# Rotary products and input sums of squares moved off GpSimd in a two-layer hybrid decoder

## The chip, the cores and the metric

The kernel runs on one core of a Trainium2 chip. A core has five engines, each with its own queue that is worked off in order: TensorE (PE: matrix products; its weight loads are shown as PEld), VectorE (DVE), ScalarE (ACT), GpSimd (POOL) and SyncE (SP), which here only issues transfers. They meet through semaphores. The metric is the device time of one execution in microseconds (us), the median of several runs.

## The reference

Sixteen learned tokens are put ahead of 1024 input tokens of width 1024 (T = 1040), all in float32. Each of two layers does this:

```python
hn = rms_norm(h, norm_mix_g[l])
proj = hn @ w_in[l]
q, k, v, xr, gate = jnp.split(proj, splits, axis=-1)
q = apply_partial_rope(rms_norm(q, q_norm_g[l]), cos, sin)
k = apply_partial_rope(rms_norm(k, k_norm_g[l]), cos, sin)
o_attn = diff_attention(q, k, v, lam)          # 4 heads x 2 components of 64, causal
o_rec = rg_lru_branch(xr, gate, ...)           # conv4, gates, linear recurrence over T
h = h + jnp.concatenate([rms_norm(o_attn), rms_norm(o_rec)], -1) @ w_out[l]
hn = rms_norm(h, norm_ffn_g[l])
h = h + (silu(g) * u) @ w_down[l]              # g, u = hn @ w_gu[l], width 2816
```

`rms_norm` divides each token by the root of the mean of its squares. `apply_partial_rope` turns the first 16 of each 64 dimensions: `x*cos` plus the swapped half times `sin`.

## The kernel before

Activations lie transposed: 128 channels on the partitions, tokens along the free dimension, eight blocks of 128 channels for the width. Work on tokens goes in three chunks of 348, 348 and 344 (`CH`). A float32 product is made from two rounded parts: a high part (`hn0h`, `wh`) and the rest (`hn0l`, `wl`), and three matmuls: high x high, low x high, high x low. `split` makes the two: ScalarE copies the high part, VectorE subtracts for the low part (with a norm weight in one instruction, line 341; without, line 323).

**The start.** `start` loads the input in nine groups (three chunks, each with blocks 0 to 2, 3 to 5 and 6 to 7) into tiles `hr`. Its inner function `group` (line 2159) splits each block into `hn0h` and `hn0l`, then squares the group's tile in place and adds its blocks together, 348 wide. What remains is summed over the channels by TensorE (`st_r`), VectorE makes the reciprocal root of it (`ms_r`, `nq_r`, `rr`), TensorE spreads it over partitions (`bc_r`), and ScalarE stores it as `row`. The first projections (`pxr`) need only `hn0h` and `hn0l`; the norm's factor is multiplied in behind them. `SQP = 2` says that chunks 0 and 1 have their squares and their sums on GpSimd; chunk 2 has squares on ScalarE and sums on VectorE.

**The recurrence** follows with `pxr` and `pgt` (x and gate branch, four blocks each) and small gate products `pga`.

**The rotation.** For each head, `qk_unit` projects a query unit and a key unit of 128 columns (`pq`, `pk`). Its `evac` (line 1008) works per chunk: ScalarE squares the result for the norm and copies it to `craw`; VectorE swaps halves into `csh` (stream shuffle, line 1024); then two products, `csh` times sine (line 1027) and `craw` times cosine (line 1028), on the engine that `ROPE_ENG` names; then VectorE adds them and the split or the key's scaling follows. There are 2 layers x 4 heads x 2 units x 3 chunks = 48 such pairs. Attention itself: TensorE makes scores (`S`), VectorE adds the mask and keeps the maximum (line 1158), ScalarE takes exponentials, VectorE combines both components, TensorE transposes (`atr`) and multiplies with the values (`pvo`). `W_ENG = "G"` puts the low parts of 70 weight halves (`wl`) on GpSimd. GpSimd also issues transfers.

**The order of the work** is set before the program is built. `Planner` runs generators against an estimated clock of each engine; an operation is written out at the moment when its generator is due, so every engine's queue follows from estimated costs (`tt`, `act`, `mm`) and from `S.turn(engine)`, which holds a generator back while that engine's estimated queue is long. Changing the engine of an operation changes the estimates, and with them the order on all engines.

Of the kernel before, what the change touches and what calls it, by code (L numbers as in the profile page):

```python
# [12 lines left out]
AF = mybir.ActivationFunctionType  # L13
ALU = mybir.AluOpType
# [10 lines left out]
CW = 348  # L25
# [55 lines left out]
NSQ, PSTAT = 3, 3  # L81

GATE_AT = 3
SQP = 2
EARLY = [6, 102]
KY = 2
NP1 = 1
# [13 lines left out]
TURN = {"w": (300.0, 3000.0), "q": (300.0, 1.0e9), "k": (0.0, 1.0e9), "v": (300.0, 300.0),  # L103
        "o": (800.0, 1.0e9), "r": (300.0, 1.0e9), "f": (300.0, 1.0e9), "d": (4000.0, 1.0e9), "s": (0.0, 1.0e9)}
DMA_RATE, DMA_END = 360.0, 900.0
ROPE_ENG, W_ENG = "G", "G"
MZ = CW
WY = [T, T, NB * P, NB * P]

# [155 lines left out]
def trunk_kernel(ctx: ExitStack, tc: tile.TileContext, h0, win, wout, wgu, wdn,  # L265
                 wgate, vec, lamd, cosd, sind, maskd, identd, seld, out):
    nc = tc.nc
    V, A, G, PE = nc.vector, nc.scalar, nc.gpsimd, nc.tensor
    S = Planner()
# [17 lines left out]
    def cols(ap):  # L287
        n = 1
        for d in ap.shape[1:]:
            n *= d  # L290
        return n

    def ready(eng, cost, after=0.0):
        return S.busy(eng, cost, after) + LAGS[eng] - LAT

    def aps(*xs):
        return sum(x is not None and not isinstance(x, (int, float)) for x in xs)

    def in_psum(ap):
        return getattr(ap, "space", None) == PSUM  # L300
# [12 lines left out]
    def act(out_, in_, func, after=0.0, **kw):  # L313
        A.activation(out=out_, in_=in_, func=func, **kw)  # L314
        n = aps(kw.get("scale"), kw.get("bias")) + ("accum_out" in kw)
        load = 0.0
        if func in TABLES and TABLES[func] != table[0]:
            table[0], load = TABLES[func], 1280.0
        m = cols(in_)
        return ready("A", max(m * 0.833 + (50 if in_psum(in_) else 93), m * 1.01 + 4) + 94 * n + load, after)  # L320

    def tt(out_, in0, in1, op, after=0.0, eng="V"):
        (V if eng == "V" else G).tensor_tensor(out=out_, in0=in0, in1=in1, op=op)  # L323
        n = cols(out_)
        if eng == "V":
            if not (in_psum(in0) or in_psum(in1)):
                after = S.behind(after)
            return ready(eng, n * 1.042 + 68, after)
        e = ready(eng, n * 2.1 + 148, after)
        S.shared.append((S.clock["G"] - n * 2.1 - 148, S.clock["G"]))  # L330
        return e
# [14 lines left out]
    def dma(eng, out_, in_, nbytes):  # L346
        eng.dma_start(out=out_, in_=in_)  # L347
        start = S.busy("G", 1040.0) + 700 if eng is G else S.busy("H", 450.0) + 770
        return S.busy("D", nbytes / DMA_RATE, start) + DMA_END
# [476 lines left out]
    def new_row(name):  # L826
        return const.pool.tile([P, TP], F32, tag="row", name=name)

    def load_vec(l):
        t = const.pool.tile([P, NVEC], F32, tag="vec", name=f"vec{l}")  # L830
        return t, dma(nc.sync if l else nc.gpsimd, t, vec[l], 512 * NVEC)
# [664 lines left out]
    def open_layer(L):  # L1496
        L.cy = open_pool(f"y{L.l}", "right")
        L.cr = open_pool(f"rec{L.l}", "right")
        L.ca = open_pool(f"attA{L.l}")
        L.accy = Acc(L.cr, L.cr.pool.tile([P, TP], F32, tag="accy", name=f"accy{L.l}"), f"accy{L.l}")  # L1500
        S.start(layer_vectors(L))
        S.set(L.ev_rec)
        S.set(L.ev_open)
# [636 lines left out]
    def start():  # L2140
        L = layers[0]
        L.vt, _ = load_vec(0)
        warm = yield from S.get(small, "d", 1, [P, 4, 4], F32, "warm")
        G.memset(warm, 0.0)
        S.free(act(warm, warm, AF.Exp), warm)
        open_layer(L)
        dma(nc.gpsimd, ident, identd, 512 * P)
        dma(nc.gpsimd, sums0, seld, 2048)
        acc = Parts(3)
        L.row = new_row("row0")  # L2150
        L.r = yield from S.get(small, "rr", 2, [BQ, NB], F32, "rr0")
        L.re = yield from S.get(small, "re", 2, [BQ, 2, NB], F32, "re0")
        _, L.ev_r, L.ev_row = row_stats(acc, KB, 1024.0, "r0", L.r, L.row, L.re)
        for b in range(KB):
            hi = yield from S.get(bpool, "b", 16, [P, T], F32R, f"hn0h{b}")
            lo = yield from S.get(bpool, "b", 16, [P, T], F32R, f"hn0l{b}")
            L.hn[b].parts = (hi, lo)

        def group(c, b0, n, tile_, there):
            t = tile_[:, :3 * CW]  # L2160
            c0, cw = CH[c]
            s = slice(c0, c0 + cw)
            for b in range(b0, b0 + n):
                yield there[b - b0]
                src = t[:, (b - b0) * CW:(b - b0) * CW + cw]
                e = yield from split(L.hn[b].parts[0][:, s], L.hn[b].parts[1][:, s], src,
                                     L.vt[:, V_MIX + b:V_MIX + b + 1])
                S.set(L.hn[b].ev[c], e + LAT)
            sq = t[:, :n * CW]
            if c < SQP:  # L2170
                e = tt(sq, sq, sq, ALU.mult, eng="G")
            else:
                yield from S.turn("A")
                e = act(sq, sq, AF.Square)
            for b in range(1, n):
                yield e + LAT
                e = tt(t[:, :CW], t[:, :CW], t[:, b * CW:(b + 1) * CW], ALU.add, eng="V" if c == 2 else "G")
            acc.put(c, b0 // 3, tile_, e + LAT)

        for c, (c0, cw) in enumerate(CH):  # L2180
            for i, (b0, n) in enumerate(((0, 3), (3, 3), (6, 2))):
                pl, tag, bufs = HR[3 * c + i]
                t = yield from S.get(L.cy if pl == "y" else L.cr, tag, bufs, [P, NB * P if pl == "y" else TP], F32,
                                     f"hr{b0}{c}")
                if cw < CW:
                    G.memset(t[:, :3 * CW].rearrange("p (b t) -> p b t", b=3)[:, :n, cw:], 0.0)
                there = []
                for a, m in ((0, 1), (1, n)) if c == 0 and i == 0 else ((0, n),):
                    e = dma(nc.sync, t[:, :3 * CW].rearrange("p (b t) -> p b t", b=3)[:, a:m, :cw],
                            h0[b0 + a:b0 + m, :, c0:c0 + cw].rearrange("b p t -> p b t"), 512 * cw * (m - a))  # L2190
                    there += [e] * (m - a)
                    if c == 0 and i == 0:
                        if not a:
                            S.start(weights())
                        yield S.now
                S.start(group(c, b0, n, t, there), there[0])
                if c == 0 and i == 2:
                    S.set(ev_x)
                    yield S.now
# [174 lines left out]
```

## Time and profile before

| | us |
|---|---|
| median of 3 timed runs | 2355.84 (2353.6 to 2357.2) |
| the profiled execution | 2362.03 |
| its span, first to last instruction | 2359.3 |
| busy: TensorE, VectorE, ScalarE, GpSimd | 2275.6, 1858.9, 1072.9, 423.1 |
| start, up to the first gate projection | 0 to 55 |
| recurrence of layer 0 | 55 to 138 |
| attention of layer 0, layer 1 | 138 to 470, 1300 to 1650 |

Times in the profile's rows are microseconds from the span's start, then the duration; in rows of groups, the busy time and the mean duration in ns. The clock of TensorE as granted is shown as a share of full speed (PEclk). Square brackets tell how long the engine stood before the row and who ended that.

### The profile page before, as it was taken

The numbers are of one execution on the slowest core, as the hardware profiler recorded it, in microseconds if no ns is written. First come the engines' busy times: TensorE is split into PE (matmuls) and PEld (weight loads), VectorE is DVE, ScalarE is ACT, GpSimd is POOL, SyncE is SP. The second block draws the span as 40 slices with busy tenths as digits, with TensorE's granted clock in tenths as the row PEclk, the third lists the DMA queues.
The fourth block names the chain that finished last, engine by engine and source line by source line (L and its number), as shares of the span: only waits on it lengthen the run. The fifth ranks groups of instructions, "written<-read, shape, count | busy, mean of one in ns | idle before, by whom it ended". The sixth has DMA issues, their size and how long they took to land.

```text
span 2359.3 us, 40740 instructions
## 1 busy us (share of the span) xinstructions
PE 2275.6 (96%) x14514; PEld 2110.9 (89%) x14514; DVE 1858.9 (79%) x4392; ACT 1072.9 (45%) x2090; POOL 423.1 (18%) x611
## 2 busy tenths in 40 slices
PE   7999899989999999999999989989899999999998
PEld 6999898989999999999999989978688888888887
DVE  7889888788888877755877988977888887776565
ACT  4656665453333333444547556644533333334432
POOL 4144333001121101000000442330012221100000
PEclk8999999999999999999999989999999999999999
DMA  3114337234565423756521143372345654238554
GB/s 123 62 39 118 103 87 254 66 122 140 202 213 182 154 93 115 250 180 211 181 93 55 56 121 83 86 252 69 113 139 205 210 189 146 98 130 290 179 189 155
DMA packets 186539, 339.36 MB, mean 144 GB/s; under 512 B 54120, under 2 KB 75290, under 8 KB 186336
## 3 DMA queue, kind: packets, MB, share of 16 engines
q1 hardware_dynamic: 153760, 227.57, 30.5%
q0 software_dynamic: 32576, 109.19, 12.7%
q8 instruction: 114, 1.87, 0.3%
q14 instruction: 89, 0.73, 0.1%
HBM read 219.72 MB, written 95.64 MB: 134 GB/s over the span
## 4 chain that ended last, share of the span: by engine, by line
PE 83%; DVE 11%; issue 2%; ACT 2%; DMA 1%; POOL 0%; SPq 0%; DVEq 0%; ACTq 0%; POOLq 0%
PE pd L304 29%; PE pb L304 16%; PE pa L304 13%; PE pxr L304 4%; PE po L304 3%; PE pgt L304 3%; PE pq L304 3%; PE pvo L304 2%; PE S L304 2%; DVE P L1158 2%; PE pk L304 2%; PE pv L304 1%; PE atr L308 1%; PE pga L304 1%; DVE P L341 1%
## 5 line engine op out<-in xcount | busy, mean ns | idle before, releaser
L304 PE MATMUL pd<-rf,wh 128*128 128x260 f32 (+1 forms) x1848 | 414.4, 319 | 0.0
L304 PEld LDWEIGHTS pd<-rf,wh 128*128 128x128 f32 x1848 | 305.7, 188 | 27.5
L304 PE MATMUL pd<-rf,wl 128*128 128x260 f32 (+1 forms) x924 | 295.9, 320 | 0.0
L347 POOL DMA_DIRECT2D ad<-ct x154 | 83.0, 540 | 577.0 <-DVE ct L323 570.5
L304 PEld LDWEIGHTS pd<-rf,wl 128*128 128x128 f32 x924 | 173.8, 188 | 13.8
L314 ACT ACTIVATE P<-P,mx,cq 116x116 f32<-116x116 f32 (+5 forms) x144 | 124.6, 867 | 79.3 <-DVE mx L341 67.6
L323 DVE TENSOR_TENSOR ct<-pd,ct 128x260 f32<-128x260 f32 (+1 forms) x204 | 102.7, 513 | 71.1 <-PE pd L304 70.9
L304 PE MATMUL pa<-B11h,fA 128*128 128x260 f32 (+1 forms) x528 | 128.4, 324 | 19.1 <-ACT B11h L314 19.1
L323 DVE TENSOR_TENSOR ct<-pb,ct 128x260 f32<-128x260 f32 (+1 forms) x198 | 101.7, 514 | 52.5 <-PE pb L304 49.0
L323 POOL TENSOR_TENSOR wl<-wr,wh 128x512 fp32r<-128x512 f32 x70 | 99.4, 1436 | 156.1 <-ACT wh L314 109.2
L304 PE MATMUL pb<-T2h,fS 128*128 128x260 f32 (+1 forms) x528 | 126.8, 322 | 0.0
L304 PE MATMUL pb<-T1h,fS 128*128 128x260 f32 (+1 forms) x528 | 126.1, 321 | 0.0
L304 PE MATMUL pa<-B21h,fA 128*128 128x260 f32 (+1 forms) x528 | 125.7, 320 | 0.4 <-ACT ct L314 0.4
L304 PE MATMUL pd<-T3h,fS 128*128 128x260 f32 (+1 forms) x528 | 126.1, 320 | 0.0
L304 PE MATMUL pb<-B22h,fS 128*128 128x260 f32 (+1 forms) x528 | 125.6, 319 | 0.0
L304 PE MATMUL pd<-T4h,fA 128*128 128x260 f32 (+1 forms) x528 | 125.2, 319 | 0.0
L323 DVE TENSOR_TENSOR ct<-ct,ct 128x520 f32<-128x520 f32 (+2 forms) x171 | 116.2, 684 | 6.5 <-DMA ad<-ct 2.8
L304 PEld LDWEIGHTS pa<-B11h,fA 128*128 128x128 f32 x528 | 90.6, 192 | 27.7 <-ACT B11h L314 19.8
L314 ACT ACTIVATE ah<-atr 116x348 fp32r<-116x348 f32 (+1 forms) x144 | 57.4, 406 | 88.6 <-PE atr L308 43.7
L304 PEld LDWEIGHTS pb<-T2h,fS 128*128 128x128 f32 x528 | 90.0, 190 | 7.8
L304 PEld LDWEIGHTS pa<-B21h,fA 128*128 128x128 f32 x528 | 88.9, 188 | 8.5 <-ACT ct L314 0.9
L304 PEld LDWEIGHTS pd<-T3h,fS 128*128 128x128 f32 x528 | 89.0, 188 | 8.0
(392 smaller groups left out, 7099.8 us busy)
## 6 DMA issues: line engine op xcount, KB each, us to landing
wr<-in_win_dram SPq DMA_DIRECT2D x80, 256.0 KB, 2.8
ad<-ct POOLq DMA_DIRECT2D x77, 260.0 KB, 2.6
ad<-ct POOLq DMA_DIRECT2D x77, 256.0 KB, 3.0
ct<-in_wgu_dram SPq DMA_DIRECT2D x64, 256.0 KB, 3.1
ht<-in_wgu_dram SPq DMA_DIRECT2D x60, 256.0 KB, 4.1
sq<-ad SPq DMA_DIRECT2D x58, 260.0 KB, 5.1
sq<-ad SPq DMA_DIRECT2D x58, 256.0 KB, 5.2
hw<-in_wgu_dram SPq DMA_DIRECT2D x48, 256.0 KB, 2.8
```

The lines of the kernel that those rows point to most:

```text
L304: PE.matmul(out_, lhsT=lhsT, rhs=rhs, start=start, stop=stop, **(dict(skip_group_check=True) if on else {}))
L308: PE.transpose(out_, in_, idn)
L314: A.activation(out=out_, in_=in_, func=func, **kw)
L323: (V if eng == "V" else G).tensor_tensor(out=out_, in0=in0, in1=in1, op=op)
L341: V.scalar_tensor_tensor(out=out_, in0=in0, scalar=s, in1=in1, op0=op0, op1=op1)
L347: eng.dma_start(out=out_, in_=in_)
L1158: V.tensor_tensor_reduce(out=pt[:mq, k0:k0 + kw], in0=sc[:mq, :kw], in1=mask, scale=1.0, scalar=NEG if i == 0 else mx[:mq, cc, i - 1:i], o ...
```

## The change

The rotation's two products go to VectorE (`ROPE_ENG`), and in `group` all squares go to ScalarE and all sums to VectorE, each behind a `turn` for that engine.

```diff
-SQP = 2
...
-ROPE_ENG, W_ENG = "G", "G"
+ROPE_ENG, W_ENG = "V", "G"
...
             sq = t[:, :n * CW]
-            if c < SQP:
-                e = tt(sq, sq, sq, ALU.mult, eng="G")
-            else:
-                yield from S.turn("A")
-                e = act(sq, sq, AF.Square)
+            yield from S.turn("A")
+            e = act(sq, sq, AF.Square)
             for b in range(1, n):
                 yield e + LAT
-                e = tt(t[:, :CW], t[:, :CW], t[:, b * CW:(b + 1) * CW], ALU.add, eng="V" if c == 2 else "G")
+                yield from S.turn("V")
+                e = tt(t[:, :CW], t[:, :CW], t[:, b * CW:(b + 1) * CW], ALU.add)
             acc.put(c, b0 // 3, tile_, e + LAT)
```

VectorE's queue in the start, from the sixth row on. `hr_124`, `hr_133` and `hr_135` are the three groups of chunk 0, `hn0l_115` to `hn0l_123` the low parts of blocks 3 to 7, `wl_139` a weight. Before:

```order
L341 SCALAR_TENSOR_TENSOR hn0l_115<-hr_133,vec_87,hn0h_114 128x348
L323 TENSOR_TENSOR wl_139<-wr_0_140,wh_138 128x512
L341 SCALAR_TENSOR_TENSOR hn0l_121<-hr_135,vec_87,hn0h_120 128x348
L323 TENSOR_TENSOR wl_139<-wr_1_142,wh_138 128x512
L341 SCALAR_TENSOR_TENSOR hn0l_117<-hr_133,vec_87,hn0h_116 128x348
L341 SCALAR_TENSOR_TENSOR hn0l_123<-hr_135,vec_87,hn0h_122 128x348
L341 SCALAR_TENSOR_TENSOR hn0l_109<-hr_144,vec_87,hn0h_108 128x348
L341 SCALAR_TENSOR_TENSOR hn0l_119<-hr_133,vec_87,hn0h_118 128x348
```

In the changed kernel:

```order
L321 TENSOR_TENSOR hr_124<-hr_124 128x348
L339 SCALAR_TENSOR_TENSOR hn0l_115<-hr_133,vec_87,hn0h_114 128x348
L321 TENSOR_TENSOR hr_124<-hr_124 128x348
L339 SCALAR_TENSOR_TENSOR hn0l_121<-hr_135,vec_87,hn0h_120 128x348
L339 SCALAR_TENSOR_TENSOR hn0l_117<-hr_133,vec_87,hn0h_116 128x348
L321 TENSOR_TENSOR wl_139<-wr_0_140,wh_138 128x512
L339 SCALAR_TENSOR_TENSOR hn0l_123<-hr_135,vec_87,hn0h_122 128x348
L321 TENSOR_TENSOR wl_139<-wr_1_142,wh_138 128x512
L339 SCALAR_TENSOR_TENSOR hn0l_119<-hr_133,vec_87,hn0h_118 128x348
L321 TENSOR_TENSOR hr_135<-hr_135 128x348
```

Sums of squares now stand between the low parts, the first of them ahead of block 3's, and block 4's low part (`hn0l_117`) has moved ahead of the weight.

VectorE's queue at the first two query chunks of layer 0 in the changed kernel (`sin_474` and `cos_473` are the tables, `hs_2` a block of the recurrence):

```order
L1022 STREAM_SHUFFLE cshq_01_1461<-crawq_01_1446 128x348
L321 TENSOR_TENSOR cshq_00_1443<-cshq_00_1443,sin_474 128x348
L321 TENSOR_TENSOR crawq_00_1399<-crawq_00_1399,cos_473 128x348
L321 TENSOR_TENSOR cshq_01_1461<-cshq_01_1461,sin_474 128x348
L321 TENSOR_TENSOR crawq_01_1446<-crawq_01_1446,cos_473 128x348
L321 TENSOR_TENSOR hs_2_1429<-hs_2_1429,gt_20_1104 128x348
```

The four products stood in GpSimd's queue before, ahead of two weight conversions:

```order
L323 TENSOR_TENSOR cshq_00_1436<-cshq_00_1436,sin_461 128x348
L323 TENSOR_TENSOR crawq_00_1404<-crawq_00_1404,cos_460 128x348
L323 TENSOR_TENSOR cshq_01_1461<-cshq_01_1461,sin_461 128x348
L323 TENSOR_TENSOR crawq_01_1448<-crawq_01_1448,cos_460 128x348
L1014 MEMSET csqq_02_1498 128x4
L323 TENSOR_TENSOR wl_1493<-wr_0_1393,wh_1492 128x512
L323 TENSOR_TENSOR wl_1493<-wr_1_1444,wh_1492 128x512
```

TensorE's queue at the first scores of head 0 in layer 0 (`S_0010`, `S_0000`), before, where they stand between the query products of head 1:

```order
L304 MATMUL pq_11_1982<-hn0l_115,wh_1655 128x348
L304 MATMUL pq_11_1982<-hn0h_114,wl_1656 128x348
L304 MATMUL S_0010_2016<-kl_0_1497,view_1836 116x116 x2
L304 MATMUL S_0000_2019<-kh_0_1496,view_1836 116x116 x2
L304 MATMUL pq_11_1982<-hn0h_116,wh_1655 128x348
```

In the changed kernel they stand 49 rows further down, between the key products of head 1:

```order
L302 MATMUL pk_10_2069<-hn0h_114,wl_1906 128x348
L302 MATMUL S_0010_2107<-kl_0_1492,view_1846 116x116 x2
L302 MATMUL S_0000_2110<-kh_0_1491,view_1846 116x116 x2
L302 MATMUL st_q_12_2114<-sums_86,csqq_12_2083 116x2 x3
L302 MATMUL pk_10_2069<-hn0h_116,wh_1905 128x348
```

TensorE's order in both feed-forward stages is the same in the two kernels.

## The prediction

> **What bounds the kernel now.** I read the chain of work that ended last, then the busy time by stage, then the timelines of the two stages that the change touches.
>
> ```profile
> PE 83%; DVE 11%; issue 2%; ACT 2%; DMA 1%; POOL 0%; SPq 0%; DVEq 0%; ACTq 0%; POOLq 0%
> ...
> core 0: us, PE busy (x) PEld busy (x) DVE busy (x) ACT busy (x) POOL busy (x), PEclk, DMA share, GB/s
> 0.00:55.00 55.00, 37.99 (x209) 35.69 (x210) 42.57 (x84) 24.18 (x44) 26.89 (x30) 0.81 0.40 130
> 55.00:138.00 83.00, 82.86 (x523) 82.58 (x522) 64.77 (x100) 59.49 (x85) 14.61 (x14) 1.00 0.16 52
> 138.00:470.00 332.00, 315.40 (x2166) 306.11 (x2164) 289.92 (x1039) 186.29 (x444) 111.92 (x141) 0.98 0.39 117
> 548.00:1196.00 648.00, 648.00 (x5409) 648.00 (x5408) 493.77 (x956) 244.84 (x455) 70.66 (x131) 1.00 0.52 175
> 1300.00:1650.00 350.00, 327.43 (x2101) 308.03 (x2101) 297.31 (x1035) 191.02 (x447) 116.28 (x142) 0.96 0.38 112
> ```
>
> TensorE sets the pace, and VectorE is the only other engine with a real share of the chain. The feed-forward stage (548 to 1196) has TensorE busy for all of its 648 us, and the change leaves its order alone. What can move is the first 55 us, where TensorE is busy for 38.0, and the two attention stages (138 to 470, 1300 to 1650), where it stands 16.6 + 22.6 = 39.2 us. Between 55 and 138 it has no gap, so a lead won before 55 is carried to 138.
>
> At the start, TensorE waits for VectorE's low halves of the input, `hn0l`:
>
> ```profile
> 11.70 0.43 PE L304 MATMUL pxr<-hn0l,wh 128*128 128x348 f32 x1 [1.80 <-DVE hn0l L341]
> 14.62 0.66 PE L304 MATMUL pxr<-hn0l,wh 128*128 128x348 f32 x1 [2.19 <-DVE hn0l L341]
> 17.19 0.66 PE L304 MATMUL pxr<-hn0l,wh 128*128 128x348 f32 x1 [1.33 <-DVE hn0l L341]
> 17.64 0.49 PE L304 MATMUL pxr<-hn0h,wl 128*128 128x348 f32 x1
> 17.93 0.49 PE L304 MATMUL pxr<-hn0h,wh 128*128 128x348 f32 x1
> ...
> 23.59 0.32 PE L304 MATMUL pxr<-hn0h,wh 128*128 128x348 f32 x1
> 23.75 0.32 PE L304 MATMUL pxr<-hn0l,wh 128*128 128x348 f32 x1
> ...
> 35.16 0.66 PE L304 MATMUL pxr<-hn0l,wh 128*128 128x348 f32 x1 [5.59 <-DVE hn0l L341]
> ...
> 39.97 0.38 PE L304 MATMUL pxr<-hn0h,wl 128*128 128x348 f32 x1
> ...
> 54.77 0.32 PE L304 MATMUL pgt<-hn0h,wh 128*128 128x348 f32 x1
> ```
>
> The waits are 1.80, 2.19, 1.33 and 5.59 us. The matmuls also show two paces: 0.29 us apart at 17.64, and 0.16 apart at 23.59 after unbroken work. After the 5.59 us gap the slow pace returns until 39.97, which is 4.8 us at about half speed. The gap thus costs its 5.59 and about 4.8 x (1 - 0.16/0.29) = 2.2 more.
>
> Why is `hn0l` late? VectorE and GpSimd side by side:
>
> ```profile
> 8.11 2.37 DVE L323 TENSOR_TENSOR wl<-wr,wh 128x512 fp32r<-128x512 f32 x1 [0.18 <-ACT wh L314]
> 10.41 1.23 DVE L341 SCALAR_TENSOR_TENSOR hn0l<-hr,vec,hn0h 128x348 fp32r<-128x348 f32 x1
> 12.90 0.57 DVE L341 SCALAR_TENSOR_TENSOR hn0l<-hr,vec,hn0h 128x348 fp32r<-128x348 f32 x1
> 13.39 0.68 DVE L323 TENSOR_TENSOR wl<-wr,wh 128x512 fp32r<-128x512 f32 x1
> 14.00 11.96 DVE L341 SCALAR_TENSOR_TENSOR hn0l<-hr,vec,hn0h 128x348 fp32r<-128x348 f32 x11
> 39.48 2.11 DVE L323 TENSOR_TENSOR hr<-hr 128x348 f32<-128x348 f32 x3
> ...
> 8.02 4.42 POOL L323 TENSOR_TENSOR hr<-hr 128x1044 f32<-128x1044 f32 x3 [4.70 <-DVE hn0l L341]
> 17.21 4.54 POOL L323 TENSOR_TENSOR hr<-hr 128x1044 f32<-128x1044 f32 x3 [0.46 <-DVE hn0l L341]
> ```
>
> The same 128x512 subtraction takes 0.68 us at 13.39 and 2.37 at 8.11, while GpSimd squares `hr`. The eleven `hn0l` from 14.00 take 11.96 us; at the 0.49 of 12.90 to 13.39 they would take 5.4. VectorE stands while GpSimd runs its two-input product. Setting each VectorE instruction against the median of its form without GpSimd beside it, 16 of them (8.11 the first, 39.48 the last) lose 16.0 us to the squares and sums.
>
> **The change at the start.** It removes all of that from GpSimd: six squares and ten sums in the first two thirds of the tokens (the last third already had its squares on ScalarE, its sums on VectorE). ScalarE gets the six squares, VectorE the ten sums:
>
> ```profile
> 7.45 0.63 ACT L314 ACTIVATE wh<-wr 128x512 fp32r<-128x512 f32 x1 [0.15 <-DMA wr<-in_win_dram]
> 8.83 0.58 ACT L314 ACTIVATE hn0h<-hr,vec 128x348 fp32r<-128x348 f32 x1 [0.75 <-DMA hr<-in_h_dram]
> ...
> L314 ACT ACTIVATE hr<-hr 128x1044 f32<-128x1044 f32 x2 | 2.2, 1078 | 4.3 <-DVE hn0l L341 4.3
> L314 ACT ACTIVATE hr<-hr 128x696 f32<-128x696 f32 x1 | 0.8, 783 | 1.2 <-DVE hn0l L341 1.2
> ...
> 243.78 0.92 DVE L323 TENSOR_TENSOR crawk<-crawk,bck 128x348 f32<-128x348 f32 x2
> ```
>
> ScalarE: 4 x 1.08 + 2 x 0.78 = 5.9 us, hidden in the 30.8 us of the first 55 in which this engine stands; without that cover each would put off the high half behind it by about its own 1.08. VectorE: two 348-wide operations together take 0.92, so one takes 0.51 alone and 0.42 behind another; ten cost 4.2 to 5.1 us against 16.0 removed. The first sum of a group now waits for ScalarE's square, with `hn0l` and weight halves queued behind it for which TensorE waits. No DMA issue of the start is moved past another.
>
> I walk the new order with these durations. ScalarE ends `wh` at 8.1, squares `hr` until 9.1, and then makes the fourth block's high half until 9.6 (it had to wait for the DMA until 8.83 anyway). VectorE does the first sum at 9.1 to 9.6, then that block's `hn0l` to 10.2: TensorE goes on at 10.3 instead of 11.70. One more sum and two `hn0l` (0.42 + 2 x 0.49) bring the next one to 11.7 instead of 14.62. Two weight subtractions (0.61 each), two `hn0l` and ScalarE's pieces between give 13.9 instead of 17.19. That is 3.3 us. From there TensorE needs 2.7 us for the 8 matmuls left of the block at 0.29 and carries on; the block on which it stood at 35.16 is made by VectorE directly behind the first rows of the norm, at about 23.5 by the same counting, and TensorE needs it at about 25.8. So the 5.59 and the 2.2 go too: 3.3 + 7.8 = 11.1. Against it: the sums of the second third are ready at about 29.4, when TensorE wants them, and VectorE stands with work behind the norm's first row until TensorE has finished its column sums. I take 1 us for these and forecast **-10 us**. Bounds: -3.3 if a gap like the fourth comes back, -12 if neither of the two costs anything.
>
> **The change in attention.** 96 products (sine and cosine, 3 chunks of 8 query and key units of both layers) go from GpSimd to VectorE:
>
> ```profile
> L323 POOL TENSOR_TENSOR wl<-wr,wh 128x512 fp32r<-128x512 f32 x70 | 99.4, 1436 | 156.1 <-ACT wh L314 109.2 <-DVE wh L335 18.5 <-DMA both<-qh 10.5
> L323 POOL TENSOR_TENSOR cshk<-cshk,sin 128x348 f32<-128x348 f32 (+1 forms) x24 | 25.7, 1069 | 51.6 <-DVE cshk L1024 14.5 <-DVE nq_q L323 8.5 <-DVE nq_k L323 5.0
> L323 POOL TENSOR_TENSOR crawq<-crawq,cos 128x348 f32<-128x348 f32 (+1 forms) x24 | 24.3, 1012 | 0.0
> ...
> 1364.14 4.60 DVE L341 SCALAR_TENSOR_TENSOR mx<-mx,cq 116x1 f32<-116x1 f32 x2
> ...
> 1364.30 1.33 POOL L323 TENSOR_TENSOR wl<-wr,wh 128x512 fp32r<-128x512 f32 x1
> 1365.54 0.99 POOL L323 TENSOR_TENSOR cshq<-cshq,sin 128x348 f32<-128x348 f32 x1
> 1366.43 0.99 POOL L323 TENSOR_TENSOR crawq<-crawq,cos 128x348 f32<-128x348 f32 x1
> 1367.32 1.33 POOL L323 TENSOR_TENSOR wl<-wr,wh 128x512 fp32r<-128x512 f32 x1
> ...
> 147.40 3.37 DVE L323 TENSOR_TENSOR hs<-hs,gt 128x348 f32<-128x348 f32 x3
> ...
> 1539.18 0.85 DVE L323 TENSOR_TENSOR nq_o<-nq_o,ox 116x3 f32<-116x3 f32 x1
> ```
>
> At 1364.14 a one-column operation stands through four GpSimd products in a row, two of them rotations: 4.6 us. By the reckoning used above, 75 VectorE instructions (147.40 the first, 1539.18 the last) lose 43.3 us to the rotations and others 53.2 to the 70 `wl` conversions, which stay. VectorE thus pays 43.3 us now for products that GpSimd makes; doing them itself costs 96 x 0.42 = 40.3 us. The difference is -3.0. Of the new work some will be caught by `wl`: VectorE now loses 53.2 in 290 + 297 us, 9%, so 40.3 would lose another 3.7. The sum on VectorE is +0.7, a wash. Each rotation also becomes about 2.06 - 0.84 = 1.2 us shorter and loses two hand-overs between engines; that helps only where a query or key is awaited, so I count -2 and forecast **-1 us** for both layers. The freed GpSimd time is hidden work and worth nothing by itself. The DMA issues on GpSimd lose the products ahead of them, and SyncE's copies of query and key blocks change places with weight loads; I price both at nothing, since TensorE's stands in these stages end mostly with VectorE, and leave them to the bounds. Bounds: -20 if half of TensorE's 39.2 us ends, +15 if VectorE's queue grows (below).
>
> A rule of the skill speaks against this sum. The Trainium skill, VectorE: DVE Perf Modes, "The DRAIN you can't avoid", says that the next operation does not start before the pipe is empty. By that rule each product would cost its whole 0.51 us, 96 x 0.51 = 49.0, and VectorE would be 5.7 us worse off instead of 3.0 better, before `wl`. The row at 243.78 has two in 0.92, so I keep 0.42.
>
> **The sum**: -10 - 1 = -11 us on the profiled execution's 2362.0, so 2351. The median of the timed runs is 2355.8, 6.2 below that execution, and the forecast for it is **2345**.
>
> **Rivals.** *More than forecast*: the freed 43.3 us of stalls lie where VectorE is the chain, and the new products in its idle time (332 - 290 + 350 - 297 = 95 us in the two stages). For it: the 4.6 us at 1364 hold up score maxima that TensorE waits for. Against: the products come at the same places as the stalls. If a quarter of the 43.3 is on the chain, 11 us more: 2334. *No change*: the lead is waited out where attention opens, since scores cannot start before the recurrence's norm is summed on a busy VectorE. For it: in the new order the first scores stand 49 rows further down TensorE's queue. Against: TensorE has no gap from 55 to 138 and its projections set when that recurrence ends. 2355. *Slower*: products at the head of VectorE's queue delay the score maxima that give TensorE its banks back, and the 70 `wl` conversions catch what the rotations caught before. Price: 49.0 - 43.3 + half of 43.3 = 27 us on VectorE; with all of it on the chain, 27 - 10 = 17 slower, with 60% of it 6 slower. It decides once VectorE's net growth passes the start's 10 us. I put it at 2364. That the change does not do what it says is ruled out: the 96 products and 15 sums stand in VectorE's new order.
>
> **Chances.** Forecast 0.58, more 0.15, no change 0.13, slower 0.14. Changes of 0.2% (4.7 us) are the least that a measurement of this kernel tells from none; a twentieth of the forecast's weight falls short of that. Faster 0.70, same 0.16, slower 0.14. The forecast's own range is 2338 to 2351; with the others the range is 2331 to 2360.
>
> **What would show it.** In the new profile: TensorE's idle time before 55 us falls from 17 to about 8, and the first gate projection, `pgt`, starts near 45 instead of 54.77; the `hn0l` all take 0.57; no VectorE instruction takes over 1.5 us beside a GpSimd product except beside `wl`; TensorE's idle time in the attention stages stays within 8 us of 39. I am wrong if the first gate projection comes less than 5 us earlier, if the lead is gone by the first feed-forward matmul, or if either attention stage grows by more than 5 us.

## The result and the profile after

| | us | ratio to before |
|---|---|---|
| before, in the comparison with the changed kernel | 2354.72 (2351.42 to 2357.2) | 1 |
| the changed kernel | 2332.69 (2331.22 to 2334.38) | 0.9896 [0.9881, 0.9911] |
| the changed kernel's profiled execution, its span | 2334.38, 2331.8 | |

The change is worth 22 us by the medians and 24.5 by the ratio, about twice the forecast 11. The new time is 12 us under the 2345 of the forecast: below the forecast's own range (2338 to 2351) and just inside the whole one (2331 to 2360). The chain of work that ended last, after:

```profile
PE 80%; DVE 13%; issue 3%; DMA 2%; ACT 2%; POOL 0%; SPq 0%; DVEq 0%; POOLq 0%; ACTq 0%
```

Busy time by stage of the changed kernel: the start, what lies between, and the attention stages of layer 0 and layer 1, these two from the first query product on: in layer 0 to the first feed-forward matmul, in layer 1 to the last output projection (`po`).

```profile
core 0: us, PE busy (x) PEld busy (x) DVE busy (x) ACT busy (x) POOL busy (x), PEclk, DMA share, GB/s
0.00:45.00 45.00, 36.46 (x217) 34.63 (x218) 30.08 (x90) 28.76 (x52) 2.90 (x14) 0.92 0.49 161
45.00:128.00 83.00, 82.32 (x520) 82.03 (x519) 63.02 (x103) 55.55 (x80) 13.48 (x14) 1.00 0.15 50
124.30:452.50 328.20, 318.80 (x2180) 312.33 (x2179) 292.96 (x1090) 190.93 (x447) 68.50 (x93) 0.97 0.39 118
1283.80:1612.00 328.20, 312.03 (x2040) 295.75 (x2040) 291.28 (x1067) 185.96 (x437) 70.48 (x94) 0.97 0.39 118
```

The same two attention stages of the kernel before, between the same pieces of work:

```profile
135.00:470.10 335.10, 318.50 (x2186) 309.21 (x2184) 292.50 (x1042) 189.38 (x447) 113.53 (x141) 0.98 0.38 116
1300.80:1639.40 338.60, 316.20 (x2028) 298.15 (x2027) 289.81 (x1014) 185.94 (x436) 116.03 (x139) 0.96 0.38 115
```

So the 27.5 us between the spans divide into 10.7 at the start (the first query product at 124.3 instead of 135.0), 6.9 in the attention of layer 0, and 10.4 in that of layer 1; the stages between moved as wholes. Not all of the 10.4 belongs to the change: the profiled execution of the kernel before was 6.2 us above its median, that of the changed kernel 1.7. A kernel with only the squares moved (below) has the order of the kernel before on every engine in layer 1, with the products on GpSimd, and there its profiled execution took 330.6 us instead of 338.6:

```profile
1301.40:1632.00 330.60, 312.48 (x2029) 295.00 (x2028) 289.24 (x1014) 185.66 (x436) 116.03 (x139) 0.97 0.39 117
```

One wait that differs is that for a copy of a query block (`both`): 4.1 us in the kernel before, 0.5 in that one, and 6.5 in the changed kernel. With 17.6 us won up to the first feed-forward matmul, some 4 to 7 of the 22 to 24.5 are left for layer 1. VectorE's busy time in attention is where it was: 292.50 to 292.96, and 289.81 to 291.28. TensorE's idle time in these two traces fell from 16.6 + 22.4 = 39.0 us to 9.4 + 16.2 = 25.6.

TensorE in the start of the changed kernel, its timeline:

```profile
10.34 0.42 PE L302 MATMUL pxr<-hn0l,wh 128*128 128x348 f32 x1 [0.19 <-DVE hn0l L339]
...
11.75 0.43 PE L302 MATMUL pxr<-hn0l,wh 128*128 128x348 f32 x1 [0.58 <-DVE hn0l L339]
...
13.94 0.66 PE L302 MATMUL pxr<-hn0l,wh 128*128 128x348 f32 x1 [0.78 <-DVE hn0l L339]
...
43.33 0.40 PE L302 MATMUL pgt<-hn0h,wh 128*128 128x348 f32 x1
```

VectorE beside it, with the first sums of squares, and the group of all low halves (busy time, mean in ns):

```profile
9.22 0.52 DVE L321 TENSOR_TENSOR hr<-hr 128x348 f32<-128x348 f32 x1 [0.54 <-ACT hr L312]
9.70 0.58 DVE L339 SCALAR_TENSOR_TENSOR hn0l<-hr,vec,hn0h 128x348 fp32r<-128x348 f32 x1
10.20 0.51 DVE L321 TENSOR_TENSOR hr<-hr 128x348 f32<-128x348 f32 x1
...
L339 DVE SCALAR_TENSOR_TENSOR hn0l<-hr,vec,hn0h 128x348 fp32r<-128x348 f32 (+1 forms) x24 | 13.1, 576 | 5.9 <-ACT hn0h L312 5.9
```

The 24 low halves take 13.1 us; before, they took 20.6. What TensorE waited for in the attention of layer 0, before and then after (us in total, times, longest):

```profile
PE atr L308 <- DVE crawk L323: 3.8, 1, 3.8
PE atr L308 <- DVE al L323: 2.7, 3, 1.4
PE S L304 <- DVE mx L1158: 2.2, 4, 1.0
PE S L304 <- DMA both<-qh: 2.0, 1, 2.0
PE st_q L304 <- POOL csqq L1014: 1.6, 1, 1.6
```

```profile
PE pvo L302 <- DVE al L321: 2.5, 1, 2.5
PE vtr L306 <- DVE ot L321: 1.2, 1, 1.2
...
PE S L302 <- DVE mx L1156: 0.3, 1, 0.3
```

The long wait behind the key's rotation is down from 3.8 to 0.3 us, and the waits for score maxima are down from 2.2 to 0.3 us in this layer. The wait for `csqq` is a small item that no term had: GpSimd clears the padding of that tile, in its queue behind products and conversions.

### The profile page after: what moved, and what is told of

It is laid out like the page before. It is cut to its first block, busy times and chain, and to the rows that moved or that the text cites. A ratio compares the mean times of both kernels' runs of the same rounds, so it can differ in the third digit from the quotient of the medians.

```text
span 2331.8 us, 40682 instructions
## 1 busy us (share of the span) xinstructions
PE 2269.1 (97%) x14514; PEld 2109.1 (90%) x14514; DVE 1845.7 (79%) x4498; ACT 1075.1 (46%) x2094; POOL 308.2 (13%) x499
## 4 chain that ended last, share of the span: by engine, by line
PE 80%; DVE 13%; issue 3%; DMA 2%; ACT 2%; POOL 0%; SPq 0%; DVEq 0%; POOLq 0%; ACTq 0%
PE pd L302 29%; PE pb L302 16%; PE pa L302 11%; PE pxr L302 3%; PE po L302 3%; PE pq L302 3%; PE pgt L302 3%; PE S L302 2%; PE pvo L302 2%; PE pk L302 2%; DVE P L1156 2%; PE pv L302 1%; PE atr L306 1%; PE pga L302 1%; DVE P L339 1%
## 5 line engine op out<-in xcount | busy, mean ns | idle before, releaser
L302 PEld LDWEIGHTS pd<-rf,wh 128*128 128x128 f32 x1848 | 305.7, 188 | 27.5
```

The costliest lines, as they stand in the source:

```text
L302: PE.matmul(out_, lhsT=lhsT, rhs=rhs, start=start, stop=stop, **(dict(skip_group_check=True) if on else {}))
```

## The experiments

All ratios are to the kernel before, with a 95% interval. Square brackets after a ratio are that interval.

### The two parts alone

The first run keeps `ROPE_ENG = "G"`, the second keeps the old `group`:

```diff
# squares only
-ROPE_ENG, W_ENG = "V", "G"
+ROPE_ENG, W_ENG = "G", "G"
# rotation only
-            yield from S.turn("A")
-            e = act(sq, sq, AF.Square)
+            if c < SQP:
+                e = tt(sq, sq, sq, ALU.mult, eng="G")
...
```

> The squares and sums of the input leave GpSimd as in the change; the rotation's products stay on GpSimd. If the start is worth what the trace of the change shows at the first gate projection (11.4 us) and the attention's gain belongs to the rotation: about 2343, TensorE's first gate projection near 43. If the rotation did nothing and all 22 us come from the start (a lead that grows in attention): about 2333.

> The rotation's products on VectorE, the input's squares and sums as before. If the two parts add up: about 11 us faster than before, near 2343, with the first gate projection near 54.8 as before and the gain in the two attention stages. If the attention's gain needs the earlier start: no change, 2354.

Measured: squares only 1.0002 [0.9983, 1.002], rotation only 0.9957 [0.994, 0.9973]. They add up to 10 us, the two together give 24. The squares alone are outside both values expected of them. With the squares alone the first query product starts at 123.1 us, 11.9 earlier than before, and the first feed-forward matmul at 470.1, as before. The stage of the squares-only kernel where the lead goes, and the same stage of a second run of it in another order (`LAT` 132, below):

```profile
123.10:470.10 347.00, 323.75 (x2180) 312.50 (x2178) 302.96 (x1042) 190.10 (x447) 114.28 (x141) 0.97 0.38 112
```

```profile
124.30:474.30 350.00, 323.82 (x2180) 313.02 (x2179) 303.44 (x1042) 190.09 (x447) 114.36 (x141) 0.97 0.37 111
```

VectorE has the same 1042 instructions as before, but they take 302.96 and 303.44 us instead of 292.50. By the reckoning of the prediction, stalls beside GpSimd grow from 42.9 to 52.3 and 52.8 us in this stage. With the lead, more of VectorE's work coincides with GpSimd's. That is 10 of the 12 to 15 us by which the stage grew; that they are its cause is likely, not shown. Behind that stage the two kernels have the same order on every engine, so a lead that is gone there is gone for good.

### Engine or order

The planner is told one engine, the products run on the other (`on` sets the engine, `eng` what is booked):

```diff
-    def tt(out_, in0, in1, op, after=0.0, eng="V"):
-        (V if eng == "V" else G).tensor_tensor(out=out_, in0=in0, in1=in1, op=op)
+    def tt(out_, in0, in1, op, after=0.0, eng="V", on=None):
+        (V if (on or eng) == "V" else G).tensor_tensor(out=out_, in0=in0, in1=in1, op=op)
...
+            e = tt(..., ALU.mult, eng=ROPE_ENG, on=ROPE_ON)
```

> The products run on VectorE, but the planner books them on GpSimd, so that TensorE's order is row for row that of the kernel with the squares alone. Theory A (VectorE's stalls beside GpSimd were on the chain, and the engine brings the gain): near the change, 2332 to 2337. Theory B (the planner's new order brings the gain): near the kernel with the squares alone, about 2343.

> The reverse: the products run on GpSimd, but the planner books them on VectorE, so that TensorE's order is row for row that of the change. Theory A (the engine): 2343 to 2348. Theory B (the order): near the change, 2333 to 2335.

Measured: products on VectorE in the order that books them on GpSimd 0.9989 [0.9973, 1.0005]; products on GpSimd in the order of the changed kernel 0.9969 [0.9955, 0.9982]. Neither engine nor order alone is worth much: the theory of the engine fails in the first run, that of the order in the second. In the second of the two, VectorE stands at the sum of the rotation, since the order puts that sum right behind products which it believes to be VectorE's own:

```profile
L322 DVE TENSOR_TENSOR crawq<-crawq,cshq 128x348 f32<-128x348 f32 (+1 forms) x24 | 16.5, 689 | 7.2 <-POOL crawq L322 7.2
L322 DVE TENSOR_TENSOR crawk<-crawk,cshk 128x348 f32<-128x348 f32 (+1 forms) x24 | 14.8, 618 | 2.8 <-POOL crawk L322 2.8
```

That is 10 us of idle time; in the kernel before these groups have none.

### Without the products

The products are booked but not made, so all else keeps its order; queries and keys stay unrotated. What a product costs on an engine is then the difference between a kernel and its floor.

```diff
-    def tt(out_, in0, in1, op, after=0.0, eng="V"):
-        (V if eng == "V" else G).tensor_tensor(out=out_, in0=in0, in1=in1, op=op)
+    def tt(out_, in0, in1, op, after=0.0, eng="V", skip=False):
+        if not skip:
+            (V if eng == "V" else G).tensor_tensor(out=out_, in0=in0, in1=in1, op=op)
...
+            e = tt(..., ALU.mult, eng=ROPE_ENG, skip=True)
```

> The changed kernel with its 96 rotary products left out (the planner still books them on VectorE, so the order of everything else on every engine is that of the changed kernel; queries and keys stay unrotated). It is the floor for this order: the changed kernel less this is what 96 products on VectorE cost, the kernel with the products on GpSimd in this order (0.9969) less this is what they cost there. Queue theory (a product on VectorE costs its own 0.42 us wherever VectorE leads): 0.978 to 0.984. Slack theory (the order has room for the products on VectorE, hardly any of their 40 us is on the path; GpSimd's stall and longer path are): 0.986 to 0.990.

> Only the input's squares moved, and the 96 rotary products left out, with the order that the planner writes when it books them on GpSimd. It is the floor for that order. Queue theory: 0.980 to 0.986, so the products cost some 30 to 45 us on either engine. Slack theory: 0.993 to 0.998, the order itself being the worse one, in which no engine for the products can help.

> The kernel before with its 96 rotary products left out (still booked on GpSimd, so all else stands in the order of before; queries and keys stay unrotated). The price of the products on GpSimd was 0.65% with the squares moved. Order theory (booking on VectorE writes a better order by itself): 0.993 to 0.996 here, and 0.004 or more below it for the order that books them on VectorE. Lead theory (the other order only spoils the lead): 0.991 to 0.995 here, and the order that books them on VectorE within 0.002 of it.

> Only the rotation moved (start as before), with its 96 products left out but booked on VectorE. By the price of the products on VectorE in the changed kernel's order (0.25%) it should give 0.993. Order theory: 0.988 to 0.991, at least 0.004 below the order of before without products. Lead theory: 0.992 to 0.995, within 0.002 of it.

Measured, with the runs above (each ratio with an interval of about 0.002 to either side):

| order books the products on, start | products on GpSimd | on VectorE | left out |
|---|---|---|---|
| GpSimd, start as before | 1 | | 0.996 |
| VectorE, start as before | | 0.9957 | 0.9929 |
| GpSimd, squares moved | 1.0002 | 0.9989 | 0.9937 |
| VectorE, squares moved | 0.9969 | 0.9896 | 0.9871 |

Three things follow. On VectorE, in the order that books them there, the products cost 0.0025 and 0.0028, some 6 us. On GpSimd they cost 0.0040 to 0.0098, 9 to 23 us. On VectorE in an order that books them on GpSimd they cost 0.0052, 12 us. And the order matters without any products: 0.0031 at the old start, where the interval just reaches nothing, and 0.0066 with the squares moved. With the squares moved both floors are where the slack theory had them. At the old start the difference of 0.0031 lies between the 0.004 of the order theory and the 0.002 of the lead theory, and does not decide between them.

The traces show where the orders part. The kernels without products, with the order for GpSimd and the squares moved, and with the order for VectorE and the old start:

```profile
124.30:461.10 336.80, 319.45 (x2180) 310.41 (x2179) 277.07 (x1042) 189.93 (x447) 65.76 (x93) 0.98 0.39 115
1293.10:1622.20 329.10, 312.71 (x2029) 295.43 (x2028) 268.35 (x1014) 186.15 (x436) 66.34 (x91) 0.97 0.40 118
```

```profile
134.50:462.90 328.40, 316.27 (x2181) 310.00 (x2180) 267.59 (x1041) 189.78 (x446) 67.38 (x93) 0.98 0.40 118
1293.60:1618.30 324.70, 309.78 (x2041) 295.80 (x2041) 268.00 (x1020) 185.44 (x437) 68.18 (x94) 0.97 0.40 120
```

With the rows of the next paragraph, the squares bring the first query product 10 us forward in either order. At the first feed-forward matmul 5.9 of them are left in the order for GpSimd (467.0 to 461.1), and 15.4 are won in the order for VectorE (462.9 to 447.5). The times say the same: 0.0023 and 0.0058, 5 and 14 us. So the order's worth lies mostly in layer 0, where it decides whether the lead is kept; in layer 1 the four stages take 324.3 to 329.1 us, which is within what two executions of one order differed by.

The traces also give VectorE's share. Attention stages of the kernel before without products, and of the changed kernel without products:

```profile
134.30:467.00 332.70, 318.86 (x2187) 311.37 (x2185) 270.58 (x1042) 189.93 (x447) 66.69 (x93) 0.97 0.39 117
1296.90:1621.20 324.30, 310.73 (x2029) 294.63 (x2028) 268.63 (x1014) 186.06 (x436) 66.03 (x91) 0.97 0.40 120
```

```profile
124.50:447.50 323.00, 313.65 (x2180) 307.98 (x2179) 269.05 (x1042) 190.88 (x447) 66.78 (x93) 0.99 0.40 120
1278.20:1602.50 324.30, 310.77 (x2040) 296.31 (x2039) 267.79 (x1019) 185.42 (x437) 68.17 (x94) 0.96 0.39 120
```

Taking the products off GpSimd frees 292.50 + 289.81 - 270.58 - 268.63 = 43.1 us of VectorE, by instructions that are not its own. Making them on VectorE takes 292.96 + 291.28 - 269.05 - 267.79 = 47.4 us. In busy time the change is a small loss. In time the 43.1 cost 9.4 us (0.0040 of 2356) and the 47.4 cost 5.9.

### One input instead of two

Each product on GpSimd becomes two passes, and in two further runs one pass, over its tile with one input (below the edit for one pass).

```diff
+        if one:
+            G.tensor_scalar(out=out_, in0=in0, scalar1=1.0, scalar2=None, op0=op)
+        else:
+            (V if eng == "V" else G).tensor_tensor(out=out_, in0=in0, in1=in1, op=op)
```

> Only the input's squares moved; in the same order, each rotary product on GpSimd is replaced by two passes over its tile with one input (times 1), so GpSimd is as long at work and the hand-overs stay, but it takes no second input (the tiles are not rotated). Stall theory (VectorE stands because of GpSimd's two-input instructions): the stalls beside the rotation fall from 47 us to under 10, and the ratio from 1.0002 to 0.990 to 0.995. Latency theory (the detour over GpSimd costs, not the stall): ratio 0.998 to 1.003.

Measured 1.0304 [1.0284, 1.0324], outside both. The run did not keep GpSimd's time: a pass takes about 1.1 us, as long as a product, and two of them twice that. VectorE stood for it at the head of its queue:

```profile
L325 DVE TENSOR_TENSOR crawq<-crawq,cshq 128x348 f32<-128x348 f32 (+1 forms) x24 | 20.0, 835 | 32.3 <-POOL crawq L323 20.0 <-POOL csqq L1016 9.3 <-POOL osq L1233 2.4
L325 DVE TENSOR_TENSOR crawk<-crawk,cshk 128x348 f32<-128x348 f32 (+1 forms) x24 | 17.8, 741 | 34.4 <-POOL crawk L323 28.9 <-POOL csqk L1016 3.4 <-POOL osq L1233 2.1
```

Idle 66.7 us in front of the 48 sums, and 71 us more time than the squares alone: the loss is about as long as this unbooked waiting at the head of the queue. GpSimd's conversions come later too, which this run does not separate. The next two runs make one pass only.

> Only the input's squares moved, in its own order; each rotary product on GpSimd is replaced by one pass with one input (times 1; the tiles are not rotated), which takes about 1.1 us there by the run with two passes, against 1.03 for the product: GpSimd's time and the hand-overs stay, VectorE's stall beside the rotation should fall from 47 us to about 8. Stall theory: 15 us between 1.0002 and the floor 0.9937 go nearly all, 0.994 to 0.996. Path theory: 0.998 to 1.002.

> The same single pass with one input on GpSimd in the changed kernel's order, where the products on GpSimd gave 0.9969 and VectorE stood 10 us at the rotation's sums for them. Stall theory: most of the 23 us above the floor 0.9871 go, 0.988 to 0.991. Path theory: VectorE still stands at the sums, 0.994 to 0.998.

Measured 0.9946 [0.9932, 0.996] and 0.9932 [0.9908, 0.9956]. In the order that books GpSimd, and by the reckoning of the prediction, the stalls beside the rotation fall from 46.9 to 17.2 us with GpSimd at work as long as before, and 13 of the 15 us above the floor go: there the price was the stall, as the stall theory had it. In the changed kernel's order the stalls fall from 33.7 to 10.6 us, but VectorE's waiting at the sums grows from 10 to 16:

```profile
L324 DVE TENSOR_TENSOR crawq<-crawq,cshq 128x348 f32<-128x348 f32 (+1 forms) x24 | 16.9, 705 | 11.9 <-POOL crawq L322 11.8
L324 DVE TENSOR_TENSOR crawk<-crawk,cshk 128x348 f32<-128x348 f32 (+1 forms) x24 | 13.7, 569 | 4.1 <-POOL crawk L322 4.1
```

The price left above that floor is 0.0061, 14 us, about those 16; the ratio lies between the two theories, with an interval that reaches into both. So there are signs of both mechanisms: a stall costs a third to a half of its length here (15 of 46.9 us, or 13 for the 29.7 by which the stalls fell), and a wait in an order that did not allow for it about all of it.

### A longer rotation

Two copies in place on ScalarE make the rotation of the changed kernel longer again without GpSimd: behind the products, or ahead of the shuffle.

```diff
             e = tt(raw[:, :cw], raw[:, :cw], L.cosT[:, c0:c0 + cw], ALU.mult, eng=ROPE_ENG)
+            A.activation(out=raw[:, :cw], in_=raw[:, :cw], func=AF.Copy)
+            A.activation(out=raw[:, :cw], in_=raw[:, :cw], func=AF.Copy)
```

> The changed kernel with the same order on every engine, but two copies of the rotated half in place on ScalarE (348 columns, about 0.45 us each and a hand-over) put between the cosine product and the sum, which makes each rotation some 1.2 us longer, as long as it was before, without GpSimd; ScalarE gets 96 copies. Latency theory (the gain beyond the forecast comes from the shorter path from a query or key to its rotation): ratio rises to 0.994 to 0.998. Stall theory (it comes from VectorE no longer standing beside GpSimd's products): ratio stays at 0.989 to 0.992.

> The changed kernel with the same two copies in place on ScalarE per rotation as in the run that gave 1.005, but directly behind ScalarE's copy of the projection, ahead of VectorE's shuffle: the same 96 copies and about the same longer path (some 0.9 us), but ScalarE no longer stands in its queue for VectorE's products. Latency theory: ratio 1.000 to 1.005 again. Queue theory (the loss came from ScalarE standing at the head of its queue, with exponentials and squares behind it): 0.990 to 0.996.

Measured 1.005 [1.0031, 1.0069] behind the products, and 0.9937 [0.9917, 0.9958] ahead of the shuffle. The first copy of each pair on ScalarE, behind the products and then ahead of the shuffle (busy, mean, idle before):

```profile
L1027 ACT ACTIVATE crawk<-crawk 128x348 f32<-128x348 f32 (+1 forms) x24 | 11.8, 494 | 36.3 <-DVE crawk L321 36.1
L1027 ACT ACTIVATE crawq<-crawq 128x348 f32<-128x348 f32 (+1 forms) x24 | 11.8, 493 | 37.0 <-DVE crawq L321 36.9
```

```profile
L1018 ACT ACTIVATE crawq<-crawq 128x348 f32<-128x348 f32 (+1 forms) x24 | 11.8, 493 | 0.8
L1018 ACT ACTIVATE crawk<-crawk 128x348 f32<-128x348 f32 (+1 forms) x24 | 11.8, 493 | 0.8
```

The first is above what either theory expected, the second is where the queue theory had it. The same 96 copies cost 27 us more where ScalarE stands 73 us in its queue for VectorE. Read alone, the first run would have passed for proof of the latency theory; the longer path is in both runs, so most of its loss was the queue. The second run costs 10 us for 47 us of work on ScalarE and about 1 us more per rotation; which of these two it pays for stays open.

### Other orders

A hand-over estimate of 132 ns instead of 130 (`LAT`) shifts the fine order and nothing else; in another run the planner books GpSimd's conversions with the mean time the trace shows.

```diff
-LAT = 130.0
+LAT = 132.0
# and in a run of its own
-        e = ready(eng, n * 2.1 + 148, after)
+        e = ready(eng, n * 2.6 + 170, after)
```

> The changed kernel, with the planner's estimate of the time from an operation to the next engine set to 132 ns instead of 130 (LAT). Every operation stays on its engine; the order shifts in some 2400 of TensorE's 11739 rows and most of VectorE's. Theory C (the planner now writes an order that fits the engine which makes the products, so both attention stages have less idle time, whatever the fine order): ratio to the kernel before 0.988 to 0.992, the two attention stages 326 to 332 us each. Theory D (the extra 11 us beyond the forecast are the luck of one order among many alike): ratio 0.993 to 1.000, with at least one attention stage above 334 us.

> The kernel before, with the same small shift of the planner's estimate (LAT 132 instead of 130). It measures how far a time moves when only the fine order does. Theory C: ratio within 0.997 to 1.003, attention stages within 4 us of 335.1 and 338.7. Theory D: ratio off 1 by 0.4% or more in either direction.

> Only the input's squares moved, with the planner's hand-over estimate at 132 ns instead of 130: another fine order of the kernel that gave 1.0002. If the start's lead is lost in attention by the mismatch of VectorE's work and its order: 0.998 to 1.004. If it was one unlucky order: 0.993 to 0.997.

> The changed kernel, with GpSimd's conversions booked by the planner at 1.50 us (2.6 ns a column and 170), the mean that the trace shows, instead of 1.22. Every operation stays on its engine. If an order that knows the engines' real times is the better one: 0.984 to 0.988. If it is one order among many alike: 0.988 to 0.995.

Measured: changed kernel 0.9919 [0.9901, 0.9937], before 1.004 [1.0019, 1.0061], squares only 1.0018 [1.0001, 1.0035], booked conversions 0.9952 [0.9936, 0.9968]. The fine order alone moves a kernel by 0.002 to 0.006, as much as the whole rotation part gave: theory D is right for the single time (1.004), theory C for the groups, though layer 0 of the changed kernel with the other estimate took 334.4 us, more than C allowed. The groups stay apart: three orders of the changed kernel lie at 0.9896, 0.9919 and 0.9952, two of the kernel before at 1 and 1.004, two with only the squares at 1.0002 and 1.0018. The mean of the three is 0.9922, 6 us above the changed kernel, so this one order is a lucky one. The mean of the two of before is 1.002, so its order was lucky as well, and the means are 0.0098 or 23 us apart: the gain as a whole does not rest on one order, as far as three and two can show. An order with truer books was not better; that theory fell.

### The conversions too

The 70 conversions left on GpSimd go to VectorE as well.

```diff
-ROPE_ENG, W_ENG = "V", "G"
+ROPE_ENG, W_ENG = "V", "V"
```

> The changed kernel, with the 70 low parts of weights that are still made on GpSimd (wl) moved to VectorE too (W_ENG). Stall theory: VectorE loses 57 us beside these 70 and pays 70 x 0.61 = 43 us to make them itself, 14 us less in sum, so the attention stages fall below 328 us each and the ratio is 0.983 to 0.988. Theory of the free engine (a product off VectorE is worth its whole VectorE time where no one waits at once): VectorE's queue grows at the places where weights come, ratio 0.990 to 0.996.

Measured 0.9943 [0.9925, 0.9962], as the theory of the free engine had it: 11 us slower than the changed kernel. The attention stages of this run:

```profile
123.50:460.50 337.00, 318.90 (x2177) 312.50 (x2176) 290.01 (x1120) 190.39 (x447) 25.58 (x63) 0.97 0.38 115
1294.00:1617.20 323.20, 306.39 (x2009) 290.75 (x2008) 279.00 (x1086) 182.91 (x430) 23.77 (x59) 0.97 0.39 116
```

VectorE's busy time over the whole execution falls from 1845.7 to 1833.9 us, 12 us, near the 14 of the stall theory. The time does not follow. Layer 0 loses 9 us. Layer 1's row is 5 us shorter, but holds 31 TensorE instructions fewer: from its first query product to the end of the span it is 1047.4 us against 1048.0. VectorE's busy time is not what these stages are paid in. No complete kernel beat the changed one.

## Why the prediction was right and wrong

**The start: right.** The walk gave TensorE's restarts at 10.3, 11.7 and 13.9; they came at 10.34, 11.75 and 13.94. The 5.59 us gap is gone, the low halves take 0.576 on average (0.57 forecast), the first gate projection came at 43.33 (near 45), TensorE's idle time in the start fell from 17.0 to 8.5 us. The start of the trace is 11.4 us shorter against 11.1 of the walk. In time the squares are worth 0.9929 - 0.9871, or 14 us with an uncertainty of 7, between the two floors of the VectorE order.

**The lead: right only together with the rotation.** The rival "no change" said that attention would wait the lead out. For the squares alone it did, wholly (1.0002). In the changed kernel it did not: the first scores stand 49 rows further down, and start only 5.8 us earlier than before, but the stage ends 17.6 earlier. By the floors, the order that books the products on VectorE keeps the lead, and the other loses part of it even without any products. The forecast added the two parts as if each kept its worth without the other.

**Attention in VectorE's time: right in the sum, in part by luck.** The reckoning had 43.3 us lost beside GpSimd's products; 43.1 came free without them. It had 40.3 + 3.7 = 44.0 us for the work on VectorE; it was 47.4. Of that, by the same reckoning, 12.3 us instead of 3.7 are more stalls beside the conversions (56.8 us, against 44.5 in the same order without products; two products are seen below, the second of them caught), so a product itself takes (47.4 - 12.3) / 96 = 0.37 us instead of 0.42. The two misses nearly cancel.

```profile
138.55 0.50 DVE L321 TENSOR_TENSOR cshq<-cshq,sin 128x348 f32<-128x348 f32 x1
138.97 1.61 DVE L321 TENSOR_TENSOR crawq<-crawq,cos 128x348 f32<-128x348 f32 x1
```

The second product starts 0.42 us after the first, which takes 0.50, so the prediction was right to keep 0.42. The rule that it weighed (the Trainium skill, VectorE: DVE Perf Modes, "The DRAIN you can't avoid") is less strict than it was put there: the same section adds that a next operation which is not held starts earlier, so this row need not contradict it.

**The step that failed** is the sentence "The sum on VectorE is +0.7, a wash", with the "-1 us for both layers" made from it. It set lost time and work against each other at one rate, and took the order around them as given. With the start as before, the rotation alone measured -10 us (0.9957; 6 to 14 by the interval) in place of -1. What the runs show of the two parts of this miss:

- The rates differ where the order is held. Stalls of 43.1 us cost 9.4 in the order for GpSimd, work of 47.4 us costs 5.9 in that for VectorE; that is -3.5 instead of -1, but each price is uncertain by about 5. In the changed kernel's order the difference is clear: the products cost 23 us on GpSimd, with 10 us of waiting at the sums, and 6 on VectorE. A stall falls on whatever VectorE has at that moment, the one-column maxima that TensorE waits for among it; booked work stands where the planner saw room. That this makes the difference is argued, not shown.
- The order was no term of the sum at all, although the prediction's own section on the kernel says that a changed engine changes the order on all engines. By the floors at the old start it is worth 0.996 - 0.9929, 7 us, uncertain by as much; with the squares moved 0.9937 - 0.9871, 15.5 us, uncertain by 7.

From the kernel before over the floors to the changed one this adds up: -9.4 (products off GpSimd) - 7.3 (order) - 13.7 (squares) + 5.9 (products on VectorE) = -24.5 us, which is 0.0104 of 2356. Another way through the same table splits it otherwise, since the parts lean on each other: with the squares first, the squares give 0, the products off GpSimd 15 and the order 15.5. The sum stands, the single terms only along their path.

**The rivals.** "More than forecast" named 2334 and came nearest (2332.7). Its price for the stalls, a quarter of 43.3, is about what was measured (9.4). It left out what the work costs (5.9) and the order (7.3), which by luck nearly outweigh each other. "Slower" did not come about: VectorE's busy time in both attention stages grew from 582.3 to 584.2 us, not by 27, and the conversions' catch is 56.8 us against 53.2 in the kernel before. That TensorE's idle time in attention would stay within 8 us of 39 was wrong (25.6), a sign that more than the start had moved.

**What stays open.** Why the order that books the products on VectorE keeps the lead through layer 0 is not settled. Orders that differ only in 2 ns of an estimate lie 0.2 to 0.4% apart, so one order each says little of a cause.

## What to carry to other kernels

Where a planner writes the order, changing an operation's engine makes two edits, and each was worth little without the other: time it with the order held, and with the work left out, before giving the gain to the engine. Busy time is no currency: work that the order had room for cost an eighth of its length here, a stall beside another engine a quarter to a half, and a wait at the head of a queue, which the order did not allow for, about all of it. Gains below about 0.5% that come through a rewritten order should be measured over several such orders.

## What was not expected of the hardware

One pass of GpSimd with one input is no faster than its product of two, but holds VectorE up far less. GpSimd's groups in the kernel with only the squares moved, and in the same order with one pass:

```profile
L321 POOL TENSOR_TENSOR cshk<-cshk,sin 128x348 f32<-128x348 f32 (+1 forms) x24 | 26.3, 1095 | 58.4 <-DVE cshk L1022 20.4 <-DVE nq_k L321 16.0 <-DVE mx L339 4.9
```

```profile
L322 POOL TENSOR_SCALAR cshk<-cshk 128x348 f32<-128x348 f32 (+1 forms) x24 | 29.6, 1231 | 55.1 <-DVE cshk L1025 20.0 <-DVE nq_k L324 15.4 <-DVE nq_q L324 5.1
```

All 96 passes together take 111.0 us against 100.0 for the products, and VectorE loses 17.2 us beside them against 46.9. The Trainium skill, SBUF — State Buffer, "SBUF: two separate sides", says that of a GpSimd instruction that reads this memory and a VectorE instruction with two inputs from it, whichever is first holds the shared pair of ports for its whole length. Beside the two-input products this case agrees, even for one-column instructions (4.60 us for two of them in the prediction's row at 1364.14); beside one-input passes VectorE loses little more than a third as much, a difference that the rule does not make.
